# Half of each last down projection by block products: chunks 3 to 6 as two units of seven products of half width

## The chip, the cores and the metric

The kernel is one program on one core of one Trainium2 chip. A core has five engines with an instruction queue each: TensorE (PE in the profile, its weight loads PEld), VectorE (DVE), ScalarE (ACT), GpSimd (POOL) and SyncE (SP, which here only issues transfers). Each queue is worked off in order; an instruction waits at the head of its queue until the semaphores that it names are there. The metric is the device time of one execution in microseconds. Three runs of the kernel before gave 1245.82 to 1248.12 us with a median of 1245.88 us.

## The reference, cut to what matters

Two decoder layers over 512 tokens of width 1024, in float32. Layer 0 mixes by a causal convolution, layer 1 by differential attention; each is followed by a SwiGLU feed-forward part (FFN) of inner width 2816 and by a gated embedding (PLE):

```python
u = rms_norm(h, ffn_norm_g[i])
h = h + (silu(u @ w_gate) * (u @ w_up)) @ w_down
gate = sigmoid(rms_norm(h, ple_norm_g[i]) @ ple_w_gate[i])
h = h + gate * (p[i] @ ple_w_proj[i])
```

The change touches the product with `w_down`, and with it how the PLE part begins.

## The kernel before, in words

**Layout.** Activations lie transposed: a tile `h[c]` holds 128 of the 1024 features in its partitions and the 512 tokens along the free axis, as do the hidden tiles. So the FFN has 22 inner chunks of 128, and every projection has 8 output chunks of 128.

**Three matmuls for one.** Float32 products are made of split operands. Each operand is a rounded part (`hi`) and a rest (`lo`), and `mm3` issues three matmuls, which are L166, L167 and L168 of the profile:

```python
T.matmul(acc, al, bh, start=first, stop=False, **kw)
T.matmul(acc, ah, bh, start=False, stop=False, **kw)
return T.matmul(acc, ah, bl, start=False, stop=last, **kw)
```

For every weight tile of 128x1024 floats there is hence a transfer of 512 KB into `wraw`, a ScalarE cast into `whi` (L159) and a VectorE subtraction into `wlo` (L161). `whi` and `wlo` have four buffers each, `wraw` two.

**The FFN in three parts.** `PARTS` cuts the 22 inner chunks into 6, 8 and 8. The 6 are made plainly. Each 8 are made by *units*: a unit makes two chunks of `u @ w_gate` or of `u @ w_up` by seven block products in place of eight (the scheme of Strassen and Winograd, 2x2 blocks: two chunks of features by two halves of 256 tokens). A unit's seven products are each 4 steps of `mm3` with 128x256 outputs, so 84 matmuls of half width. It needs sums of weight blocks (S1 to S4: four POOL operations of 128x512, L729, L730, L741 and L742) and sums of activation blocks (T1 to T4, made once per layer in `Operands.chunk`). `Unit.prep` makes and splits the weight operands (L719/L720 for two at a time, L745/L746 for S3), `Unit.p` issues a product and drains it. A unit's last two products, 4 and 3, are issued among the next unit's first ones. An up unit's hidden chunks are multiplied with the gate and split into `hid` (L803, L808, L810, L811).

**Down projections.** After each part, `linear` adds `hid @ w_down` to `h`: 8 output chunks, each 8 steps of `mm3` over the part's inner chunks (24 matmuls of 128x512), drained by one VectorE addition from PSUM into `h` (L890). During those of parts 0 and 1 the next part's first unit is prepared; during that of part 2 there is nothing more to prepare, and each finished `h[m]` goes to `Norm.chunk`: a scaled split on ScalarE and VectorE (L206, L207), a square on ScalarE (L225, L228) and its addition to `acc` on POOL (L229).

**PLE.** `ple` makes 8 chunks of 24 matmuls over `norm.u`. After the norm's column sums (L199) and a small chain on VectorE and POOL, two matmuls (L291) spread the token factors over the partitions; ScalarE copies them to `rb` (L262), and only then the first PLE accumulator can be drained (L921, then ScalarE's sigmoid L922). There are four PSUM accumulators `mm`, so the fifth PLE chunk waits for the first drain. `pp`, the eight tiles of `p[i] @ ple_w_proj[i]`, are made well before the FFN and multiplied in at L923.

**What sets the order.** The program is written in the order of the mathematics, and a scheduler, by a timeline of its own, decides the order of each engine's queue. `tc.issue_after` keeps an instruction behind another, and inside `tc.manual_schedule` the written order holds.

Of the kernel before, what the change touches and what calls it, by code (L numbers as in the profile page):

```python
# [91 lines left out]
def trunk(ctx, tc, xT, pT, wts, diag, dww, vec, rel, onehot, lamv, out):  # L92
# [116 lines left out]
    class Norm:  # L209


        def __init__(self, g, acc_engine=None):
            self.g, self.u = g, []
            self.eng = acc_engine or G

        def split(self, c):
            hi, lo = both(sb([P, 2, S], f"A{c}", 1, F32R))
            split_scaled(h[c], col(self.g, c), hi, lo)
            self.u.append((hi, lo))

# [327 lines left out]

    pp = []
    pw = [weight(), weight()]  # L550

# [109 lines left out]
    class Operands:  # L661

        def __init__(self, norm, spare):
            self.norm = norm
            self.tops, self.uppers, lowers = spare()
            self.low = []
            for j in range(2):
                lh, ll = lowers(j)
                self.low += [(lh[:, i], ll[:, i]) for i in range(2)]
            self.at = {n: [None] * 4 for n in ("B11", "B21", "B22", "T1", "T2", "T3", "T4")}  # L670

        def chunk(self, k, rb):
# [13 lines left out]
            V.tensor_tensor(t[:, 3], u21, t[:, 1], ALU.subtract)  # L686
            hi, lo = self.tops(k)
            A.copy(hi, t)
            V.tensor_tensor(lo1, u11, f(hi1), ALU.subtract)
# [8 lines left out]
    class Unit:  # L698
# [9 lines left out]
        def load(self):  # L708
# [6 lines left out]
            self.s3 = sb([P, 2, S], f"A{6 + self.n % 2}", 1)[:, 0]  # L715

        def two(self, src, a, b):
            hi, lo = sb([P, 2, S], "whi", 4, F32R), sb([P, 2, S], "wlo", 4, F32R)
            A.copy(hi, src)  # L719
            V.tensor_tensor(lo, src, f(hi), ALU.subtract)  # L720
            for j, n in enumerate((a, b)):
                self.w[n] = hi[:, j], lo[:, j]

        def prep(self, step):
# [15 lines left out]
            elif step == 3:  # L740
                G.tensor_tensor(s3, r0[:, 0], r1[:, 0], ALU.subtract)  # L741
                G.tensor_tensor(r1[:, 0], r0[:, 1], s[:, 1], ALU.subtract)  # L742
            elif step == 4:
                hi, lo = both(sb([P, 2, S], f"A{4 + self.n % 2}", 1, F32R))
                A.copy(hi, s3)  # L745
                V.tensor_tensor(lo, s3, f(hi), ALU.subtract)  # L746
                self.w["S3"] = hi, lo
            else:
                self.two(r1, "S4", "A22")
# [7 lines left out]
        def p(self, i):  # L757
# [7 lines left out]
            }[i]  # L765
            self.product(acc, w, b, first)
            o = self.out
            if i == 1:
# [6 lines left out]
            elif i == 7:  # L775
                A.copy(o[1][:, HT:], a)
                V.tensor_tensor(o[1][:, HT:], o[1][:, HT:], lo, ALU.add)
                self.ready(1, 1)
# [15 lines left out]
    class Up(Unit):  # L794
        def start(self):
            self.out = wk(), wk()
            self.done = [0, 0]

        def ready(self, j, k):
# [9 lines left out]
            hid = both(sb([P, 2, S], f"B{self.at + j}", 1, F32R))  # L809
            A.copy(hid[0], o)  # L810
            V.tensor_tensor(hid[1], o, f(hid[0]), ALU.subtract)  # L811
            self.hid[self.at + j] = hid

    def ffn(norm, after, spare):
        rb = None
        ops = Operands(norm, spare)

        def units(n, hid):
            us = []
            for i in range(0, n, 2):  # L820
                g, u = Gate(2 * (i // 2), i == 0, "A"), Up(2 * (i // 2) + 1, False, "wraw")
                g.hid = hid
                u.gate, u.at, u.hid = g, i, hid
                us += [g, u]
# [3 lines left out]

        def run(us):
            for n, x in enumerate(us):  # L830
# [6 lines left out]
                if nxt:  # L837
                    nxt.prep(0)
                x.p(2)
                if nxt:  # L840
                    nxt.prep(1)
                if last:
                    last.p(4)
                x.p(6)
                if nxt:
                    nxt.prep(2)
                if last:
                    last.p(3)
                x.p(5)
                if nxt:  # L850
                    nxt.prep(3)
                    nxt.prep(4)
                x.p(7)
                if nxt:
                    nxt.prep(5)
            us[-1].p(4)
            us[-1].p(3)

        us = None
        for at, (f0, n) in enumerate(PARTS):  # L860
# [28 lines left out]
            def add(m, acc):  # L889
                V.tensor_tensor(h[m], acc, h[m], ALU.add)  # L890
                if at == len(PARTS) - 1:
                    after.chunk(m)

            hooks = {}
            if at < len(PARTS) - 1:
                n2 = PARTS[at + 1][1]
                now = wnext[0]
                wnext[0] += NC
                us = units(n2, [None] * n2)
# [47 lines left out]
    n2 = Norm("ple_g0")  # L947
    ffn(norm, n2, spare0)
    norm = Norm("attn_g")
# [323 lines left out]
    n2 = Norm("ple_g1")  # L1273
    ffn(norm, n2, spare1)

# [32 lines left out]
def _layout(a):  # L1308
# [12 lines left out]
    def ffn(i):  # L1321
        g, u = _stationary(a["ffn_w_gate"][i]), _stationary(a["ffn_w_up"][i])
        r = []
        for f0, n in PARTS:
# [3 lines left out]
            for c in range(f0 + plain, f0 + n, 2):  # L1328
                r += [g[c], g[c + 1], u[c], u[c + 1]]
            r += list(pad(_stationary(a["ffn_w_down"][i][f0 * P : (f0 + n) * P])))  # L1330
        return r
# [78 lines left out]
```

## Time and profile before

| | |
|---|---|
| median of 3 runs | 1245.88 us |
| the profiled execution | 1246.42 us, its span 1244.7 us |
| TensorE busy | 1232.4 us, 99% of the span, 7080 matmuls |
| TensorE weight loads | 1080.8 us, 87% |
| VectorE busy | 882.1 us, 71% |
| ScalarE busy | 623.8 us, 50% |
| GpSimd busy | 471.1 us, 38% |
| granted TensorE clock | 1.000 |

The last down projection of layer 0 runs from about 504 to 551 us of the span, and that of layer 1 about 644 us later. A row of a timeline reads: start, duration, engine, line, operation, written tile, read tiles, shape, count, and in brackets how long the engine had been idle and what released it. Names are given without their numbers, so all eight PLE accumulators are `mm`. Matmul durations overlap: what a matmul costs a busy TensorE is the distance from its start to the next one's start.

### The profile page before, as it was taken

How to read it: one execution, taken by the hardware profiler on the slowest of the kernel's cores; microseconds unless marked ns; L12 is line 12 of the kernel's file. 1: busy time of each engine (PE TensorE's matmuls, PEld its weight loads, DVE VectorE, ACT ScalarE, POOL GpSimd, SP SyncE). 2: the span in 40 equal slices, each digit the busy share in tenths (PEclk: the TensorE clock that was granted, in tenths of full speed). 3: DMA queues.
4: the chain of work that ended last, by engine and by line, in shares of the span. 5: the costliest groups of instructions: out<-in, count | busy, mean ns of one | idle time of the engine just before them, and what ended most of it. 6: DMA issues, size and time to landing. Idle time of an engine off the chain costs nothing.

```text
span 1244.7 us, 18430 instructions
## 1 busy us (share of the span) xinstructions
PE 1232.4 (99%) x7080; PEld 1080.8 (87%) x7080; DVE 882.1 (71%) x1242; ACT 623.8 (50%) x1096; POOL 471.1 (38%) x355
## 2 busy tenths in 40 slices
PE   9999999999999999999999999999999999999998
PEld 7888788888998899888888888788889998999887
DVE  6998866885895479547676876646966885587535
ACT  5653464443553255434566877735434552455432
POOL 3863442024670364133346645041026650552120
PEclk9999999999999999999999999999999999999999
DMA  7566213334233322334332331143333333232331
GB/s 267 177 210 193 90 51 119 98 98 127 86 102 118 102 86 71 117 104 149 126 113 76 112 90 38 52 144 93 89 122 95 103 111 112 83 102 86 104 100 67
DMA packets 49154, 136.33 MB, mean 110 GB/s; under 512 B 5635, under 2 KB 10243, under 8 KB 49068
## 3 DMA queue, kind: packets, MB, share of 16 engines
q1 hardware_dynamic: 46944, 131.74, 34.0%
q10 hardware_dynamic: 2124, 3.43, 0.9%
q8 instruction: 55, 0.90, 0.3%
q14 instruction: 31, 0.25, 0.1%
HBM read 128.84 MB, written 6.31 MB: 109 GB/s over the span
## 4 chain that ended last, share of the span: by engine, by line
PE 88%; DVE 4%; issue 2%; DMA 1%; ACT 0%; SPq 0%; POOL 0%; DVEq 0%; ACTq 0%
PE mm L166 27%; PE mm L167 27%; PE mm L168 27%; PE mm L1126 1%; DVE sc L458 1%; PE sc L1094 1%; PE sc L1093 1%; PE tp L1113 1%; PE sc L407 1%; PE mm L407 1%; PE tp L1047 1%; PE mm L363 1%; PE tp L199 1%; DVE wlo L720 0%; DVE wlo L161 0%
## 5 line engine op out<-in xcount | busy, mean ns | idle before, releaser
L159 ACT CAST whi<-wraw 128x1024 fp32r<-128x1024 f32 (+2 forms) x145 | 145.7, 1014 | 229.0 <-PE mm L168 110.9
L161 DVE TENSOR_TENSOR wlo<-wraw,whi 128x1024 fp32r<-128x1024 f32 (+2 forms) x141 | 180.4, 1285 | 82.0 <-ACT whi L159 79.7
L166 PE MATMUL mm<-A,wlo 128*128 128x512 f32 (+1 forms) x568 | 220.4, 388 | 1.1 <-ACT A L206 1.0
L167 PE MATMUL mm<-A,whi 128*128 128x512 f32 (+1 forms) x568 | 219.2, 387 | 0.0
L168 PE MATMUL mm<-A,whi 128*128 128x512 f32 (+1 forms) x568 | 217.3, 389 | 0.0
L166 PE MATMUL mm<-B,wlo 128*128 128x512 f32 x352 | 137.0, 389 | 0.0
L167 PE MATMUL mm<-B,whi 128*128 128x512 f32 x352 | 137.0, 389 | 0.0
L168 PE MATMUL mm<-B,whi 128*128 128x512 f32 x352 | 135.6, 389 | 0.0
L229 POOL TENSOR_TENSOR acc<-acc,wk 128x512 f32<-128x512 f32 x35 | 60.0, 1715 | 190.6 <-ACT wk L228 189.9
L166 PEld LDWEIGHTS mm<-A,wlo 128*128 128x128 f32 x568 | 106.8, 188 | 23.7 <-ACT A L206 1.3
L167 PE MATMUL mm<-C,whi 128*128 128x256 f32 x448 | 126.8, 283 | 0.0
L168 PE MATMUL mm<-C,whi 128*128 128x256 f32 x448 | 126.8, 283 | 0.0
L166 PE MATMUL mm<-C,wlo 128*128 128x256 f32 x448 | 126.8, 283 | 0.0
L168 PEld LDWEIGHTS mm<-A,whi 128*128 128x128 f32 x568 | 106.5, 188 | 21.9 <-issue 0.5
L167 PEld LDWEIGHTS mm<-A,whi 128*128 128x128 f32 x568 | 106.7, 188 | 21.1
L720 DVE TENSOR_TENSOR wlo<-A,whi 128x1024 fp32r<-128x1024 f32 x60 | 106.2, 1778 | 19.7 <-ACT whi L719 19.6
L719 ACT CAST whi<-A 128x1024 fp32r<-128x1024 f32 x60 | 62.9, 1049 | 55.5 <-PE mm L168 44.3
L729 POOL TENSOR_TENSOR A<-A 128x512 f32<-128x512 f32 x16 | 25.7, 1606 | 165.5 <-DMA A<-in_wts 156.7
L729 POOL TENSOR_TENSOR A<-wraw 128x512 f32<-128x512 f32 x16 | 24.7, 1546 | 167.4 <-DMA wraw<-in_wts 152.7
L167 PEld LDWEIGHTS mm<-C,whi 128*128 128x128 f32 x448 | 86.0, 192 | 0.2
L166 PEld LDWEIGHTS mm<-C,wlo 128*128 128x128 f32 x448 | 86.0, 192 | 0.2
L168 PEld LDWEIGHTS mm<-C,whi 128*128 128x128 f32 x448 | 86.0, 192 | 0.0
(314 smaller groups left out, 3031.6 us busy)
## 6 DMA issues: line engine op xcount, KB each, us to landing
wraw<-in_wts SPq DMA_DIRECT2D x161, 512.0 KB, 3.6
A<-in_wts SPq DMA_DIRECT2D x32, 512.0 KB, 3.6
wraw<-in_wts SPq DMA_DIRECT2D x16, 384.0 KB, 3.1
D<-in_diag SPq DMA_DIRECT2D x22, 256.0 KB, 4.8
C<-in_diag SPq DMA_DIRECT2D x16, 256.0 KB, 4.8
h<-in_xT SPq DMA_DIRECT2D x8, 256.0 KB, 5.5
rest<-h SPq DMA_DIRECT2D x8, 256.0 KB, 2.5
bias<-scr ACTq DMA_DIRECT2D x8, 256.0 KB, 3.6
```

Of the source, the lines that this page charges most:

```text
L159: A.copy(hi[:, cut], raw[:, cut])
L161: eng.tensor_tensor(lo[:, cut], raw[:, cut], f(hi[:, cut]), ALU.subtract)
L166: T.matmul(acc, al, bh, start=first, stop=False, **kw)
L167: T.matmul(acc, ah, bh, start=False, stop=False, **kw)
L168: return T.matmul(acc, ah, bl, start=False, stop=last, **kw)
L199: r = T.matmul(t[:, cut], src[:, cut], ones, start=first and b == 0, stop=last and b == 3)
L229: self.last = self.eng.tensor_tensor(self.acc, self.acc, sq, ALU.add)
L363: last_tap[0] = T.matmul(acc, dg[:, j % 4], ups[c][:, j : j + S], start=(j == 0), stop=(j == PE_TAPS[c] - 1))
L407: last_tap[0] = T.matmul(acc[:, g * P : (g + 1) * P], w, ups[c][:, g, LEAD - m : LEAD - m + P], start=(m == 0), stop=(m == LAGS - 1),)
L719: A.copy(hi, src)
L720: V.tensor_tensor(lo, src, f(hi), ALU.subtract)
L729: G.tensor_tensor(s[:, 0], r1[:, 0], r1[:, 1], ALU.add)
```

## The change

Only the third part's down projection of each layer changes.

- Output chunks 0, 1, 2 and 7 are made as before, 24 matmuls of 128x512 each. Chunks 3 and 4, and 5 and 6, are made by one `Down` unit each: seven products of 12 matmuls, 128x256.
- The activation operands are the hidden chunks of part 2 and their block sums. For these the up units of part 2 write their float hidden values where `pp` lay. POOL makes the sums of three of the four chunk pairs (12 operations of 128x256, L924 to L927 of the changed kernel), VectorE those of the fourth (4 operations). Eight ScalarE casts (L933) and eight VectorE subtractions (L934), all 128x512, split them into the tiles of the earlier T1 to T4.
- The weight operands are made as for any unit: two raw tiles, four sums on POOL, four pairs of operands per unit.
- After products 1, 6 and 7, ScalarE copies the accumulator to a `big` tile (L847), since the next product reuses the bank, and VectorE adds it from there to `h` (L920); after the others VectorE adds straight from PSUM.
- `pp` is stored to DRAM after part 0 (8 transfers of 256 KB, L1043) and fetched again behind the second unit's weights (8 of 256 KB, L989).
- PLE reads its operands in the order 0, 1, 2, 7, 3, 4, 6, 5.

The core of the diff:

```diff
+    pps = [[dram.tile([P, S], F32, tag=f"pp{i}{m}", name=f"pp{i}{m}") for m in range(NC)] for i in range(2)]
...
     class Up(Unit):
         def start(self):
-            self.out = wk(), wk()
+            self.out = self.pp[self.at : self.at + 2] if self.pp else (wk(), wk())
...
+    class Down(Unit):
+        def __init__(self, n, m, b, add, done, homes):
+            super().__init__(n, False, None)
+            self.m, self.b, self.add, self.done = m, b, add, done
+            self.homes = homes
+
+        def load(self):
+            self.raw = []
+            r, s, s3, self.thirds = self.homes
+            for j in range(2):
+                raw = sb([P, 2, S], *r[j])
+                self.fetched = nc.sync.dma_start(raw, wts[self.i + j].rearrange("p (j k) -> p j k", j=2))
+                self.raw.append(raw)
+            self.sums = sb([P, 2, S], *s)
+            self.s3 = sb([P, 2, S], *s3)[:, 0]
+
+        def third(self):
+            if len(self.thirds) == 1:
+                return both(sb([P, 2, S], *self.thirds[0], F32R))
+            return [sb([P, S], *t, F32R) for t in self.thirds]
+
+        def start(self):
+            pass
+
+        def drain(self, i, a, lo, hi):
+            t1, t2 = slice(0, HT), slice(HT, S)
+            if i in (1, 6, 7):
+                o = big()[:, :HT]
+                A.copy(o, a)
+            for j, cut, src in {
+                1: lambda: ((0, t1, o),), 2: lambda: ((0, t1, hi),), 6: lambda: ((0, t2, o),), 5: lambda: (),
+                7: lambda: ((1, t2, o), (1, t2, lo)), 4: lambda: ((1, t1, a),), 3: lambda: ((0, t2, lo),),
+            }[i]():
+                self.add(self.m + j, cut, src)
+            if i in (4, 3):
+                self.done(self.m + (i == 4))
...
+        def down(hid, up):
+
+            base = wnext[0]
+            ws = [weight() for _ in range(2)]
+            b = {n: [None] * 4 for n in ("T1", "T2", "T3", "T4")}
+            for n, j, k in (("B11", 0, 0), ("B21", 1, 0), ("B22", 1, 1)):
+                b[n] = [tuple(t[:, k * HT : (k + 1) * HT] for t in hid[2 * i + j]) for i in range(4)]
+
+            def add(m, cut, src):
+                V.tensor_tensor(h[m][:, cut], src, h[m][:, cut], ALU.add)
+
+            def sums(k, eng):
+                (u11, u12), (u21, u22) = ((u[:, :HT], u[:, HT:]) for u in pp[2 * k : 2 * k + 2])
+                eng.tensor_tensor(u22, u22, u12, ALU.subtract)
+                eng.tensor_tensor(u12, u12, u11, ALU.subtract)
+                eng.tensor_tensor(u11, u11, u22, ALU.add)
+                eng.tensor_tensor(u21, u21, u11, ALU.subtract)
+
+            def split(k, i):
+                hi, lo = ops.tiles[k]
+                two = slice(2 * i, 2 * i + 2)
+                src = pp[2 * k + i].rearrange("p (j t) -> p j t", j=2)
+                A.copy(hi[:, two], src)
+                V.tensor_tensor(lo[:, two], src, f(hi[:, two]), ALU.subtract)
+                for j, n in enumerate((("T2", "T1"), ("T4", "T3"))[i]):
+                    b[n][k] = hi[:, 2 * i + j], lo[:, 2 * i + j]
+
+            one = lambda t: (t, 1)
+            xs = [
+                Down(0, 3, b, add, after.chunk, ((one("A6"), one("A3")), one("A4"), one("A7"), (one("A5"),))),
+                Down(1, 5, b, add, after.chunk, ((("wraw", 2),) * 2, one("A6"), one("A3"), (("wth", 2), ("wtl", 2)))),
+            ]
+            x = xs[0]
+            with tc.issue_after(up.last_sum.ins):
+                for k in range(3):
+                    sums(k, G)
+            for i in range(2):
+                xs[i].i = base + 4 + 2 * i
+            wnext[0] = base + 2
+            ws += [weight(), weight()]
+            x.load()
+            x.prep(1)
+            x.prep(3)
+            with behind(up.seventh), tc.manual_schedule(engines={V.engine, A.engine}):
+                for k in range(3):
+                    split(k, 0)
+            with behind(up.ends), tc.manual_schedule(engines={V.engine, A.engine}):
+                sums(3, V)
+                split(3, 0)
+                for k in range(4):
+                    split(k, 1)
+            with behind(up.ends):
+                x.prep(0)
+
+            def plain(ms, ws):
+                accs = [mm() for _ in ms]
+                for k in range(NC):
+                    for w_, a_ in zip(ws, accs):
+                        mm3(a_, wpart(w_, k), hid[k], k == 0, k == NC - 1)
+                for m, a_ in zip(ms, accs):
+                    add(m, slice(0, S), a_)
+
+            plain((0, 1), ws)
+            with behind(x.ends):
+                x.prep(2)
+            for m in range(2):
+                after.chunk(m)
+            plain((2,), ws[2:])
+            with behind(x.ends):
+                x.prep(4)
+                x.prep(5)
+            after.chunk(2)
+            plain((7,), ws[3:])
+            after.chunk(7)
+            wnext[0] = base + 8
+            run(xs, x.ends)
+            with tc.issue_after(xs[1].fetched.ins):
+                for m in range(NC):
+                    nc.sync.dma_start(pp[m], pps[m])
+            after.order = 0, 1, 2, 7, 3, 4, 6, 5
...
-            linear(n, hid, add, 2, at=hooks)
             if hooks:
+                linear(n, hid, add, 2, at=hooks)
                 wnext[0] = end
+            else:
+                down(hid, us[-1])
+            if at == 0:
+                for m in range(NC):
+                    nc.sync.dma_start(pps[m], pp[m])
...
-                for k in range(NC):
-                    mm3(acc, wpart(w, k), tuple(t[:, cut] for t in norm.u[k]), k == 0, k == NC - 1)
+                for k in norm.order:
+                    mm3(acc, wpart(w, k), tuple(t[:, cut] for t in norm.u[k]), k == norm.order[0], k == norm.order[-1])
...
+            if f0 + n == FC:
+                halves = w[3:7].reshape(4, P, 4, 2, P).transpose(0, 1, 3, 2, 4).reshape(4, P, 1024)
+                w = np.concatenate([w[:3], w[7:], halves])
```

How the queues stand afterwards is decided by the scheduler. Three places of layer 0, first in VectorE's queue, from the drain of plain chunks 0 and 1 to the first operand of the second Down unit. `mm_4851` and `mm_4852` are those two accumulators, `wlo_4848`, `wlo_4904` and `wlo_4948` operands of the first Down unit, `wlo_5013` the operand A11 and A12 of the second.

```order
430 L920 TENSOR_TENSOR h_7_87<-mm_4851,h_7_87 128x512
431 L920 TENSOR_TENSOR h_8_88<-mm_4852,h_8_88 128x512
432 L724 TENSOR_TENSOR wlo_4848<-A_750_4811,whi_4847 128x1024
433 L724 TENSOR_TENSOR wlo_4904<-A_752_4815,whi_4903 128x1024
434 L920 TENSOR_TENSOR h_9_89<-mm_4918,h_9_89 128x512
435 L750 TENSOR_TENSOR A_765_4944<-A_753_4816,A_765_4944 128x512
436 L207 SCALAR_TENSOR_TENSOR A_760_4907<-h_7_87,vec_63,A_760_4907 128x512
437 L207 SCALAR_TENSOR_TENSOR A_762_4912<-h_8_88,vec_63,A_762_4912 128x512
438 L724 TENSOR_TENSOR wlo_4948<-A_751_4813,whi_4947 128x1024
439 L207 SCALAR_TENSOR_TENSOR A_768_4951<-h_9_89,vec_63,A_768_4951 128x512
440 L920 TENSOR_TENSOR h_14_94<-mm_4957,h_14_94 128x512
441 L724 TENSOR_TENSOR wlo_5013<-wraw_4989,whi_5012 128x1024
```

Before, the two drains were followed by two weight splits (L161), one drain, three L207 and one more weight split. Now two 128x1024 splits and one 128x512 split are added ahead of `wlo_5013`, which the 25th matmul after the plain chunks reads.

GpSimd's queue at the same place. L733, L734, L745 and L746 are the weight sums (L729, L730, L741 and L742 of before), first of the first Down unit (`A_752` and its neighbours), then of the second (`A_775`, `A_776`, `wraw_4991`); L229 is the norm's sum of squares.

```order
158 L745 TENSOR_TENSOR A_753_4816<-A_750_4811,A_751_4813 128x512
159 L927 TENSOR_TENSOR D_255_1375<-D_255_1375,D_239_1301 128x256
160 L734 TENSOR_TENSOR A_752_4815<-A_752_4815,A_750_4811 128x512
161 L746 TENSOR_TENSOR A_751_4813<-A_750_4811,A_752_4815 128x512
162 L733 TENSOR_TENSOR A_775_4993<-wraw_4991 128x512
163 L734 TENSOR_TENSOR A_775_4993<-A_775_4993,wraw_4989 128x512
164 L229 TENSOR_TENSOR acc_4910<-acc_4910,wk_4915 128x512
165 L229 TENSOR_TENSOR acc_4910<-acc_4910,wk_4954 128x512
166 L745 TENSOR_TENSOR A_776_4994<-wraw_4989,wraw_4991 128x512
167 L746 TENSOR_TENSOR wraw_4991<-wraw_4989,A_775_4993 128x512
168 L229 TENSOR_TENSOR acc_4910<-acc_4910,wk_4986 128x512
```

Before, the L229 additions stood directly behind the last up unit's sums; now 12 activation sums and two units' weight sums stand between and among them. Row 162 writes the tile pair of `A_750`, so it waits for VectorE's row 432.

TensorE's queue at the spread (L291) of the PLE norm of layer 0, before. `mm_5173` is the third PLE accumulator, `mm_5215` the fourth; the fifth, `mm_5257`, begins 24 matmuls after the second spread, at row 2947.

```order
2918 L166 MATMUL mm_5173<-A_792_5056,wlo_5169 128x512
2919 L291 MATMUL tp_5142<-wk_5106,ones_70 128x512
2920 L167 MATMUL mm_5173<-A_792_5056,whi_5168 128x512
2921 L168 MATMUL mm_5173<-A_792_5056,whi_5168 128x512
2922 L291 MATMUL tp_5142<-wk_5108,ones_70 128x512
2923 L166 MATMUL mm_5215<-A_754_4822,wlo_5211 128x512
```

And now, where `mm_5398` is the fourth accumulator and `mm_5440` the fifth.

```order
3015 L167 MATMUL mm_5398<-A_801_5231,whi_5393 128x512
3016 L168 MATMUL mm_5398<-A_801_5231,whi_5393 128x512
3017 L291 MATMUL tp_5325<-wk_5289,ones_70 128x512
3018 L291 MATMUL tp_5325<-wk_5291,ones_70 128x512
3019 L166 MATMUL mm_5440<-A_760_4907,wlo_5436 128x512
```

The chunk of 24 matmuls that stood behind the spread stands ahead of it, and the fifth accumulator follows the spread directly. Layer 1 is ordered alike at these three places.

More of the change, by code (lines that the diff above doesn't have):

```diff
@@ L809, in ready, with third, drain, ffn @@
             hid = both(sb([P, 2, S], f"B{self.at + j}", 1, F32R))
[L810 to L811 removed]
+            self.ends = A.copy(hid[0], o), V.tensor_tensor(hid[1], o, f(hid[0]), ALU.subtract)
             self.hid[self.at + j] = hid
[L814 removed]
+    class Down(Unit):
[12 more added lines that the diff above has]
+            self.s3 = sb([P, 2, S], *s3)[:, 0]
+        def third(self):
+            if len(self.thirds) == 1:
[3 more added lines that the diff above has]
+            pass
+        def drain(self, i, a, lo, hi):
+            t1, t2 = slice(0, HT), slice(HT, S)
[9 more added lines that the diff above has]
+                self.done(self.m + (i == 4))
+    def ffn(norm, after, spare, pp, pps):
         rb = None
         ops = Operands(norm, spare)
[L818 removed]
+        def units(n, hid, last):
             us = []
@@ L827, in units, with run, prep @@
             return us
-        def run(us):
+        def run(us, ends=()):
+            def prep(x, n):
+                with behind(ends):
+                    x.prep(n)
             for n, x in enumerate(us):
```

49 lines of the change are left out of this document (27 added, 22 removed).

## The prediction

> **What bounds the kernel now.** I read the page's busy times and chain of waits first, then the stretches around the last down projection of layer 0, then the timelines there.
>
> ```profile
> span 1244.7 us, 18430 instructions
> PE 88%; DVE 4%; issue 2%; DMA 1%; ACT 0%; SPq 0%; POOL 0%; DVEq 0%; ACTq 0%
> 480.00:505.00 25.00, 25.00 (x207) 24.87 (x206) 19.58 (x24) 15.07 (x26) 7.39 (x4) 1.00 0.27 82
> 505.00:530.00 25.00, 25.00 (x124) 21.15 (x123) 14.66 (x18) 9.81 (x14) 3.28 (x2) 1.00 0.33 104
> 530.00:560.00 30.00, 30.00 (x138) 25.01 (x137) 13.64 (x17) 11.30 (x16) 11.44 (x8) 1.00 0.36 108
> PE sc L407 <- DMA C<-pi: 1.7, 1, 1.7
> ```
>
> The chain is TensorE's. The stretches give busy times of PE, PEld, DVE, ACT and POOL, then the clock: TensorE is busy for all of all three, and the longest wait of the whole run is 1.7 us. So a matmul less is time saved, and any wait put into TensorE's queue here is time lost. From 505 to 560 us VectorE, ScalarE and POOL are half idle, with slack that nothing used. That slack is what the change spends.
>
> **Part 1: the matmuls.** Per layer, 4 x 24 matmuls of width 512 become 2 x 84 of width 256.
>
> ```profile
> 479.91 0.28 PE L168 MATMUL mm<-wtl,whi 128*128 128x256 f32 x1
> 480.03 0.28 PE L166 MATMUL mm<-C,wlo 128*128 128x256 f32 x1
> 534.47 0.69 DVE L890 TENSOR_TENSOR h<-mm,h 128x512 f32<-128x512 f32 x1 [1.53 <-PE mm L168]
> 539.91 0.69 DVE L890 TENSOR_TENSOR h<-mm,h 128x512 f32<-128x512 f32 x1 [2.42 <-PE mm L168]
> ```
>
> Half-width matmuls start 0.12 us apart; VectorE's drains follow each plain chunk 5.44 us apart. A unit takes 84 x 0.12 = 10.08 us in place of 2 x 5.44 = 10.88 us: 0.80 saved, **-1.6 us per layer**. The nearest rows are those of the up units, with the same shapes; nothing would be saved only if the matmuls started 10.88/84 = 0.13 us apart. [...] The rows are 0.227 and 0.12, and I keep to them.
>
> **Part 2: the second Down unit's first operand.** This is the largest term. The second unit's product 1 stands 24 half-width matmuls behind plain chunk 7. Chunk 7 is the fourth chunk and ends where the fourth does now, 534.47 - 5.44 = 529.0; TensorE arrives at 529.0 + 24 x 0.12 = 531.9. It needs `wlo_5013`, row 441 of VectorE's new queue. The rows before:
>
> ```profile
> 514.48 0.69 DVE L811 TENSOR_TENSOR B<-wk,B 128x512 fp32r<-128x512 f32 x1
> 521.10 1.37 DVE L890 TENSOR_TENSOR h<-mm,h 128x512 f32<-128x512 f32 x2 [5.93 <-PE mm L168]
> 522.39 2.35 DVE L161 TENSOR_TENSOR wlo<-wraw,whi 128x1024 fp32r<-128x1024 f32 x2
> 524.65 0.69 DVE L890 TENSOR_TENSOR h<-mm,h 128x512 f32<-128x512 f32 x1
> 525.25 4.15 DVE L207 SCALAR_TENSOR_TENSOR A<-h,vec,A 128x512 fp32r<-128x512 f32 x3
> 479.44 0.68 DVE L746 TENSOR_TENSOR A<-A,A 128x512 fp32r<-128x512 f32 x1
> 487.16 1.45 DVE L746 TENSOR_TENSOR A<-A,A 128x512 fp32r<-128x512 f32 x1
> 494.20 1.22 DVE L720 TENSOR_TENSOR wlo<-A,whi 128x1024 fp32r<-128x1024 f32 x1
> 482.44 4.47 DVE L720 TENSOR_TENSOR wlo<-A,whi 128x1024 fp32r<-128x1024 f32 x2
> 482.30 1.29 POOL L729 TENSOR_TENSOR A<-wraw 128x512 f32<-128x512 f32 x1 [4.80 <-DVE wlo L720]
> 483.56 2.27 POOL L741 TENSOR_TENSOR A<-wraw,wraw 128x512 f32<-128x512 f32 x1
> 488.15 1.62 POOL L742 TENSOR_TENSOR wraw<-wraw,A 128x512 f32<-128x512 f32 x1
> 525.50 3.36 POOL L229 TENSOR_TENSOR acc<-acc,wk 128x512 f32<-128x512 f32 x2 [35.74 <-ACT wk L228]
> ```
>
> VectorE and POOL slow each other: a 128x1024 split takes 1.22 alone and 2.24 beside POOL (4.47 for two), a 128x512 one 0.68 and 1.45, and of the three L207 two stand beside POOL's 3.36 us (at 0.75 for the free one, (4.15 - 0.75)/2 = 1.70 each). POOL's 1.29 becomes 2.27. Additions from PSUM keep 0.69.
>
> VectorE's new work behind the last up unit (free at 514.48 + 0.69) is four 128x256 sums and five 128x512 splits with ScalarE's casts ahead, about 4 x 0.47 + 0.7 + 5 x 0.61 = 5.6 us, with three earlier splits before it (1.8 us) that only partly fit; the drains of 521.10 start about 1.2 us late, at 522.3 (0 to 1.2). From there to the start of `wlo_5013`, start to start and undisturbed: two drains 1.29, two splits 2.26, drain 0.60, split 0.60, two L207 1.34, split 1.14, L207 0.67, drain 0.61, so 8.5 us, to 530.8; the split ends at 532.0. That is a wait of 0.2 us, the low end. Disturbed: POOL may start its row 162 when row 432 is read, at 524.7, and then has 2.27 + 2.27 + 2 x 1.68 + 2.27 + 1.62 = 11.8 us of work, to 536.5. From 524.7 VectorE needs 2.24 + 0.60 + 1.37 + 2 x 1.70 + 2.24 + 1.70 + 0.61 + 2.27 = 14.4 us: 539.1, a wait of 7.2 us, the high end. POOL's list fills 11.8 of the 14.4 us, but its rows 164 and 166 wait for ScalarE and VectorE, so I take three quarters of the way: **+5.4 us**. The cover that fails is VectorE's idle time: it was 2.42 us per chunk, and is gone.
>
> [...]
>
> **Part 3: a copy on the path.** In the first unit product 4 follows product 7 on the same bank, with ScalarE's copy (L847) between. A copy waits for a matmul's end, and product 4 for the copy.
>
> ```profile
> 504.76 0.37 ACT L776 COPY wk<-mm 128x256 f32<-128x256 f32 x1
> 375.08 0.41 DVE L777 TENSOR_TENSOR big<-big,mm 128x256 f32<-128x256 f32 x1
> 375.54 0.39 PE L166 MATMUL mm<-wth,wlo 128*128 128x256 f32 x1 [0.21 <-DVE big L777]
> ```
>
> The last matmul's 0.28 us, some 0.04, the copy's 0.37, 0.05 until TensorE starts (375.49 to 375.54), less the 0.12 that a spacing takes anyway: 0.62 us. A 128x1024 cast of PLE's weight (about 1 us) stands ahead of the copy in ScalarE's queue, so up to 1.6. I take **+1.0 us**.
>
> **Part 4: the fifth PLE accumulator.** It needs the first one's bank, and that needs `rb`. Now 24 matmuls (5.44 us) cover the chain behind the spread:
>
> ```profile
> 568.04 0.39 PE L291 MATMUL tp<-wk,ones 128*128 128x512 f32 x1
> 568.29 1.05 ACT L159 CAST whi<-wraw 128x1024 fp32r<-128x1024 f32 x1 [4.61 <-PE mm L168]
> 569.25 0.58 ACT L262 COPY rb<-tp 128x512 f32<-128x512 f32 x1
> 569.37 1.23 DVE L161 TENSOR_TENSOR wlo<-wraw,whi 128x1024 fp32r<-128x1024 f32 x1 [4.44 <-ACT whi L159]
> 570.52 1.88 DVE L921 TENSOR_TENSOR big<-mm,rb 128x512 f32<-128x512 f32 x3
> ```
>
> In the new order the chunk stands ahead of the spread. From the start of its last matmul: its end 0.39, the cast from 0.43 (its buffer is freed there), `rb` 0.96 later and 0.58 long, VectorE's split 1.08 behind the cast's start, at 1.51, the drain 1.15 later at 2.66, done at 3.35, TensorE at 3.40. Three spacings (0.68) would have passed anyway: **+2.7 us**; without cast and split ahead 1.2, with one more small job 3.
>
> **Part 5: the last up unit.** POOL's twelve new sums now lie beside VectorE's last up unit.
>
> ```profile
> 497.07 0.41 DVE L777 TENSOR_TENSOR big<-big,mm 128x256 f32<-128x256 f32 x1
> 499.82 0.28 PE L166 MATMUL mm<-wth,wlo 128*128 128x256 f32 x1
> ```
>
> That drain frees the bank which the matmul at 499.82 needs: 2.3 us to spare. Right ahead of it in VectorE's queue stand two 128x1024 and two 128x512 instructions with two SBUF inputs; disturbed like those of part 2 they take 2 x 1.02 + 2 x 0.77 = 3.6 us more. POOL's new jobs are half as wide and leave gaps, so I take three quarters, 2.8: **+0.5 us**, between 0 and 1.3.
>
> **At nothing:** the transfers of `pp`,
>
> ```profile
> rest<-h SPq DMA_DIRECT2D x8, 256.0 KB, 2.5
> wraw<-in_wts SPq DMA_DIRECT2D x161, 512.0 KB, 3.6
> ```
>
> which take 2.5 us each beside weights of 3.6 us. The stores pass on SP between loads with waits of their own; the eight loads stand ahead of PLE's first weight, some 20 us before its use, and `pp` itself is read only after 570 us. Without that cover they would cost a few transfers' time. Rows of the attention part that the scheduler sets a little differently: 0, between -1 and +2.
>
> **Sum:** -1.6 + 5.4 + 1.0 + 2.7 + 0.5 = +8.0 us per layer, +16.0 for both. The profiled execution took 1246.4 us and would take 1262.4; the median lies 0.5 below it, so **1262 us**.
>
> **The rivals.** About 0.2% (2.5 us) is what a measurement can tell from no change.
>
> *A. VectorE and POOL find room* (0.16). Part 2 is 0.2, part 5 nothing: -1.6 + 0.2 + 1.0 + 2.7 = +2.3, 1250.5 us. For it: L207 beside no POOL job took 0.75. Against it: in the 480 to 490 us stretch, with POOL's list as dense, every split was slowed. Its lower end, with the small ends of parts 3 and 4, is +0.4, 1246.7 us: no change (0.05 more).
>
> *B. Faster, TensorE waits for nothing* (0.07). The operands come before TensorE, because VectorE, half idle from 505 to 560 us, starts the splits earlier than I count, and the first PLE bank is free at the spread: -1.6 per layer, 1242.7 us. It decides from waits under 0.35 us a layer in all (-1.6 + 0.35 = -1.25, twice that is -2.5). Against it: parts 3 and 4 follow from the order alone.
>
> *C. The clock falls behind the wait* (0.12). At its start TensorE was slow after idling:
>
> ```profile
> 1.52 4.21 PE L141 MATMUL tp<-ones,ident 128*128 128x128 f32 x18 [1.52 <-POOL ident masks.py:199]
> 6.20 1.05 PE L199 MATMUL tp<-ones,wk 128*128 128x128 f32 x8
> ```
>
> 0.23 us a piece, against 0.13 later. A wait of 5.4 us, three times the longest of the trace, may bring that back: 4.2 us at half pace lose 2.1, so 10.1 per layer, 1266 us. The clock stood at 1.00 throughout, so nothing here shows it. [...]
>
> *D. POOL never pauses* (0.08), and each wait is at its high end: 7.2 + 1.6 + 3.0 + 1.3 - 1.6 = 11.5 per layer, 1269 us. For it: the dense rows of 480 to 490 us; against it, POOL's own waits.
>
> **How the numbers follow.** The forecast has 0.52. Faster: B and a rest, 0.08. Same: 0.06. Slower: A to D without these, 0.86. From 1248 to 1270 us stand the forecast and A, C and D, 0.87 before I allow for sizes taken from neighbouring rows, some 0.8 after it; B and no change stay out.
>
> **What would show it.** Right: a wait of 4 to 7 us of TensorE for VectorE's L724 some 28 us behind the last up unit in each layer, with those splits at 2.2 us; one near 1 us for L847; one of 2.7 us for L1057 right behind L291. Half-width matmuls 0.12 us apart show part 1. Wrong: no wait over 1 us at L724 (A or B), or matmuls behind it at twice the spacing (C).

## The result, and the profile after

The changed kernel takes 1267.08 us (median of 5 runs, 1265.73 to 1267.86) against 1246.4 us of the kernel before on the same chip: ratio 1.0164, 95% interval 1.0152 to 1.0177, slower by 20.7 us by the medians, 20.4 by the ratio. The profiled execution's span grew from 1244.7 to 1265.6 us, by 20.9. The forecast was 1262, the range 1248 to 1270.

The page's first line, and of the view of waits the rows on TensorE that are new (line waited at, what for; us in total, times, longest):

```profile
span 1265.6 us, 18932 instructions
PE mm L166 <- DVE wlo L724: 7.8, 2, 3.9
PE mm L166 <- DVE big L1057: 5.2, 2, 2.6
PE mm L166 <- ACT big L847: 1.7, 2, 0.8
```

The three waits of the forecast stand there, each once per layer; no other wait of their size is new. TensorE's timeline of layer 0 shows them from start to start:

```profile
531.65 0.28 PE L168 MATMUL mm<-B,whi 128*128 128x256 f32 x1
535.76 0.58 PE L166 MATMUL mm<-B,wlo 128*128 128x256 f32 x1 [3.82 <-DVE wlo L724]
536.14 0.41 PE L167 MATMUL mm<-B,whi 128*128 128x256 f32 x1
536.35 0.41 PE L168 MATMUL mm<-B,whi 128*128 128x256 f32 x1
...
545.15 0.28 PE L168 MATMUL mm<-C,A 128*128 128x256 f32 x1
546.28 0.39 PE L166 MATMUL mm<-C,wlo 128*128 128x256 f32 x1 [0.84 <-ACT big L847]
...
579.18 0.61 PE L291 MATMUL tp<-wk,ones 128*128 128x512 f32 x2
582.39 0.80 PE L166 MATMUL mm<-A,wlo 128*128 128x512 f32 x1 [2.59 <-DVE big L1057]
582.98 0.63 PE L167 MATMUL mm<-A,whi 128*128 128x512 f32 x1
583.41 0.63 PE L168 MATMUL mm<-A,whi 128*128 128x512 f32 x1
```

The second Down unit's product 1 starts 4.10 us (531.65 to 535.76) behind the matmul ahead of it, 3.98 more than a spacing of 0.12. Behind that, half-width matmuls start 0.21 us apart, and behind the fifth PLE accumulator's wait full-width ones 0.43 apart, where 0.12 and 0.227 were measured at full clock. Three stretches of the first place follow, each with its length, TensorE's busy time (and its matmuls), the granted clock, and the share and GB/s of the transfers:

```profile
532.00:536.00 4.00, 0.24 (x1) 0.75 0.00 0
536.00:538.00 2.00, 2.00 (x10) 0.50 0.31 27
542.00:545.00 3.00, 3.00 (x27) 1.00 0.00 0
```

The granted clock averages 0.75 over the wait, is 0.50 behind it, and 1.00 again in the last stretch. The trace's record of it has the fall at 534.03 us and the rise at 540.86. So a wait here costs twice: while TensorE stands, and while it works at half pace afterwards. The account by the starts of the matmuls, in us:

| | layer 0 | layer 1 |
|---|---|---|
| matmuls saved (2 units x 0.80) | -1.6 | -1.6 |
| wait for L724 (second unit, product 1) | 4.0 | 4.1 |
| half pace behind it (24 and 28 spacings) | 2.3 | 2.7 |
| wait for L847 (copy between products 7 and 4) | 1.1 | 1.1 |
| wait for L1057 (fifth PLE accumulator) | 2.75 | 2.8 |
| half pace behind it (7 and 8 spacings) | 1.4 | 1.7 |
| last up unit | 0 | 0 |
| sum | 10.0 | 10.8 |

Together 20.8, against 20.9 by the spans. The attention part in between added nothing that can be seen.

### The profile page after: what moved, and what is told of

Its sections match the earlier page's. It is cut to its first block, busy times and chain, and to the rows that moved or that the text cites. A ratio compares the mean times of both kernels' runs of the same rounds, so it can differ in the third digit from the quotient of the medians.

```text
span 1265.6 us, 18932 instructions
## 1 busy us (share of the span) xinstructions
PE 1238.6 (98%) x7224; PEld 1092.0 (86%) x7224; DVE 921.6 (73%) x1294; ACT 641.8 (51%) x1132; POOL 527.6 (42%) x395
## 5 line engine op out<-in xcount | busy, mean ns | idle before, releaser
L159 ACT CAST whi<-wraw 128x1024 fp32r<-128x1024 f32 (+2 forms) x137 | 137.2, 1011 | 185.2 <-PE mm L168 70.8
L161 DVE TENSOR_TENSOR wlo<-wraw,whi 128x1024 fp32r<-128x1024 f32 (+2 forms) x133 | 173.4, 1310 | 71.1 <-ACT whi L159 70.7
L166 PE MATMUL mm<-C,wlo 128*128 128x256 f32 x496 | 141.2, 285 | 1.7 <-ACT big L847 1.7
L167 PE MATMUL mm<-C,whi 128*128 128x256 f32 x496 | 140.9, 284 | 0.0
L168 PE MATMUL mm<-C,whi 128*128 128x256 f32 x496 | 140.8, 284 | 0.0
L166 PE MATMUL mm<-B,wlo 128*128 128x512 f32 (+1 forms) x336 | 127.9, 381 | 7.8 <-DVE wlo L724 7.8
L724 DVE TENSOR_TENSOR wlo<-A,whi 128x1024 fp32r<-128x1024 f32 x68 | 115.6, 1710 | 20.6 <-ACT whi L724 20.5
L167 PE MATMUL mm<-B,whi 128*128 128x512 f32 (+1 forms) x336 | 127.3, 379 | 0.0
L168 PE MATMUL mm<-B,whi 128*128 128x512 f32 (+1 forms) x336 | 125.9, 379 | 0.0
L229 POOL TENSOR_TENSOR acc<-acc,wk 128x512 f32<-128x512 f32 x35 | 55.9, 1598 | 129.9 <-ACT wk L228 129.3
L733 POOL TENSOR_TENSOR A<-wraw 128x512 f32<-128x512 f32 x18 | 28.0, 1558 | 196.4 <-DMA wraw<-in_wts 152.8
L724 ACT CAST whi<-A 128x1024 fp32r<-128x1024 f32 x68 | 71.1, 1048 | 57.2 <-PE mm L168 50.1
L166 PEld LDWEIGHTS mm<-C,wlo 128*128 128x128 f32 x496 | 95.9, 193 | 2.4 <-ACT big L847 2.1
L167 PEld LDWEIGHTS mm<-C,whi 128*128 128x128 f32 x496 | 95.8, 193 | 0.3
L733 POOL TENSOR_TENSOR A<-A 128x512 f32<-128x512 f32 x18 | 29.3, 1630 | 160.0 <-DMA A<-in_wts 159.4
L168 PEld LDWEIGHTS mm<-C,whi 128*128 128x128 f32 x496 | 95.7, 193 | 0.0
```

The costliest lines, as they stand in the source:

```text
L159: A.copy(hi[:, cut], raw[:, cut])
L161: eng.tensor_tensor(lo[:, cut], raw[:, cut], f(hi[:, cut]), ALU.subtract)
L229: self.last = self.eng.tensor_tensor(self.acc, self.acc, sq, ALU.add)
L724: self.ends = A.copy(hi, src), V.tensor_tensor(lo, src, f(hi), ALU.subtract)
L733: G.tensor_tensor(s[:, 0], r1[:, 0], r1[:, 1], ALU.add)
```

## The experiments

My theory after the result: three waits, all made by the order and load of VectorE's and ScalarE's queues, and a clock that falls when TensorE stands long enough. The rivals: matmuls that are slow for another reason (operands, banks); a VectorE queue that is too long whatever POOL does; waits that only move when one of them is cleared. In the diffs below `...` stands for lines that are not shown, and the comments explain them.

### Does idling slow TensorE? Needless matmuls in the gaps

```diff
+NF1, NF2 = 17, 11
...
+    def filler(n):
+        t = tp()
+        for _ in range(n):
+            r = T.matmul(t, ones_r, fill_src[0], start=True, stop=True)
+        return r
...
+                    with tc.issue_after(last.second.ins):
+                        filled = filler(NF1)         # ahead of the second Down unit's product 1
+                    with tc.issue_after(filled.ins):
+                        x.p(1)
...
+                with tc.issue_after(last_spread[0].ins):
+                    filled = filler(NF2)             # behind the spread
```

With both:

> 17 needless 128x512 matmuls stand ahead of the second Down unit's product 1, and 11 behind the spread, in each layer; the operands come as late as before. If TensorE's pace behind the waits is lost because it stood idle, the waits of VectorE's chain stay but the matmuls behind them start 0.12 and 0.227 us apart: about 2.5 us less at the first place and 1.5 at the second, twice, so some 8 us off the changed kernel's 1267: 1259. If the slow matmuls have another cause (their operands or their banks), the time stays at 1267 or grows by what the needless matmuls are too many, up to 1 us.

Measured: 1262.1 us, ratio 1.0126 (1.0108 to 1.0145), 5 us under the changed kernel and 3 over what was expected. The matmuls behind both filled gaps ran at full pace. But the scheduler had also put the first unit's product 5 further forward, and it now waited for a drain of VectorE, 2.27 us in each layer. The row of TensorE's timeline in layer 0 and the stretch behind it:

```profile
539.54 0.39 PE L167 MATMUL mm<-C,wlo 128*128 128x256 f32 x1 [2.11 <-DVE h L937]
540.00:542.00 2.00, 2.00 (x12) 0.50 0.02 6
```

In layer 0 that wait brought the clock down again; in layer 1 the same wait (2.39 us from start to start) did not. In the profile the miss is thus 2.27 us twice in place of L847's 1.1, and 1.7 us of half pace once: 2 x 1.2 + 1.7 = 4.1. By the median it is 3.1; the profiled execution, 1263.9 us, is the slowest of four, and two of the others show a mean granted clock of 1.000, so the fall did not come in each. To have the order of the changed kernel untouched, only the second filler was kept:

```diff
-NF1, NF2 = 17, 11
+NF1, NF2 = 0, 11
```

> Of the needless matmuls only the 11 behind the spread stand, in each layer; the rest of TensorE's queue is that of the changed kernel. If idling lowers the pace, the fifth PLE accumulator's matmuls start 0.227 us apart and not 0.43, the wait itself stays: 1.5 us less in layer 0 and 2 in layer 1, 1263.5. If the slow matmuls there come from their operands or banks, they stay slow and the time stays at 1267.

Measured: 1262.9 us, ratio 1.0133 (1.0119 to 1.0146). The timeline behind the spread, layer 0:

```profile
579.08 2.65 PE L705 MATMUL tp<-A,ones 128*128 128x512 f32 x11
581.86 0.50 PE L167 MATMUL mm<-A,wlo 128*128 128x512 f32 x1
582.19 0.40 PE L168 MATMUL mm<-A,whi 128*128 128x512 f32 x1
582.43 0.39 PE L169 MATMUL mm<-A,whi 128*128 128x512 f32 x1
```

The fifth accumulator starts as late as before, 2.8 us behind the spread, but its matmuls are 0.24 apart at once. In the run before it was the same, so behind this filler the clock stood in 4 of 4 cases. The same matmuls on the same operands and bank: it was the idling. The ratios lie 0.0031 apart, 3.9 us, where 1.5 + 2 were expected. Not all of it is the filler's: at the first place, left as it was, half pace cost 1.4 us a layer in this profile and not 2.3 and 2.7.

### Is it POOL that makes the operand late?

```diff
+                w = slice(0, 16 if self.g in ("ple_g0", "ple_g1") else S)
-                self.last = self.eng.tensor_tensor(self.acc, self.acc, sq, ALU.add)
+                self.last = self.eng.tensor_tensor(self.acc[:, w], self.acc[:, w], sq[:, w], ALU.add)
...
+            if self.n == 1:      # sums come from a transfer, POOL writes 16 columns of them
+                nc.sync.dma_start(self.sums, wts[self.i].rearrange("p (j k) -> p j k", j=2))
+                nc.sync.dma_start(self.s3, wts[self.i, :, 0:S])
```

> POOL's weight sums of the second Down unit and the PLE norms' sums of squares are made on 16 of 512 columns (the other columns of the weight sums come from a transfer, the other squares are left out); VectorE's queue is in the same order. If POOL's work is what slows VectorE, its splits take 1.2 and 0.7 us, the 4.0 us wait for L724 falls to 0 to 0.3, and with it the 2.5 us of half pace: 13 us off in two layers, 1254. If the queue is too long by itself, the wait loses less than 1 us and the time stays above 1264.

This kernel leaves out most of both sums and shows times alone. Measured: 1254.4 us, ratio 1.0074 (1.0054 to 1.0094). VectorE's timeline of the changed kernel:

```profile
521.95 1.28 DVE L920 TENSOR_TENSOR h<-mm,h 128x512 f32<-128x512 f32 x2
523.14 2.35 DVE L724 TENSOR_TENSOR wlo<-A,whi 128x1024 fp32r<-128x1024 f32 x2
...
526.01 1.19 DVE L750 TENSOR_TENSOR A<-A,A 128x512 fp32r<-128x512 f32 x1
527.12 3.48 DVE L207 SCALAR_TENSOR_TENSOR A<-h,vec,A 128x512 fp32r<-128x512 f32 x2
530.52 2.31 DVE L724 TENSOR_TENSOR wlo<-A,whi 128x1024 fp32r<-128x1024 f32 x1
532.76 0.74 DVE L207 SCALAR_TENSOR_TENSOR A<-h,vec,A 128x512 fp32r<-128x512 f32 x1
...
534.02 1.68 DVE L724 TENSOR_TENSOR wlo<-wraw,whi 128x1024 fp32r<-128x1024 f32 x1
```

and POOL's beside it:

```profile
524.49 2.16 POOL L733 TENSOR_TENSOR A<-wraw 128x512 f32<-128x512 f32 x1 [14.11 <-DVE wlo L724]
526.73 1.62 POOL L734 TENSOR_TENSOR A<-A,wraw 128x512 f32<-128x512 f32 x1
528.31 3.44 POOL L229 TENSOR_TENSOR acc<-acc,wk 128x512 f32<-128x512 f32 x2
532.91 1.71 POOL L745 TENSOR_TENSOR A<-wraw,wraw 128x512 f32<-128x512 f32 x1 [1.16 <-DVE wlo L724]
```

The same part of VectorE's queue with POOL's work cut to 16 columns:

```profile
526.33 1.41 DVE L207 SCALAR_TENSOR_TENSOR A<-h,vec,A 128x512 fp32r<-128x512 f32 x2
527.66 1.22 DVE L725 TENSOR_TENSOR wlo<-A,whi 128x1024 fp32r<-128x1024 f32 x1
...
530.06 1.22 DVE L725 TENSOR_TENSOR wlo<-wraw,whi 128x1024 fp32r<-128x1024 f32 x1
```

Two L207 take 1.41 us and not 3.48, a split 1.22 and not 2.31, and the late operand is done at 531.3 and not 535.7. The order of VectorE's queue is the same. No wait at product 1 in layer 0, 0.3 us in layer 1, full pace behind it. The wait at product 1 and its share of half pace, 13.1 us in both layers by the account and 12.6 by the times, need POOL's work beside VectorE's.

### Two changes of order alone

The PLE chunk behind the spread again:

```diff
+            if m == 2:
+                return tc.issue_after(columns.ins)        # third accumulator behind the column sums
+            return tc.issue_after(last_spread[0].ins) if m == 3 else nullcontext()
```

> The PLE's third accumulator is put behind the column sums and the fourth behind the spread, so that 24 matmuls stand again between the spread and the fifth accumulator. If the fifth accumulator's wait came from that order alone, the 2.75 us wait and the 1.5 us of slow matmuls behind it go: 8.5 us off, 1258.5. If the chain behind the column sums is then too short of cover, a wait of 1 to 3 us appears at the spread instead, and the time stays above 1262.

Measured: 1259.4 us, ratio 1.0108 (1.0093 to 1.0123). The wait for L1057 and its half pace are gone in both layers, and 0.87 us of waiting in each appeared earlier, at PLE's first accumulator for its last operand (L207).

VectorE's queue eased, with POOL's work as it was:

```diff
-            for m in range(2):
-                after.chunk(m)
...
+            def mid(ins):                 # called behind the second unit's last operands
+                with tc.issue_after(ins.ins):
+                    for m in (0, 1, 2, 7):
+                        after.chunk(m)
```

> The norm's VectorE splits of chunks 0, 1, 2 and 7 (L207) are queued behind the second Down unit's last operands. VectorE then reaches the late operand about 2.5 us earlier: the wait falls from 4.0 to 1.5 us, too short to slow TensorE by the theory of the clock, so 2.5 + 2.5 us less per layer, 10 in all, less some 0.3 of new waits for copies: 1257.5. If the pace falls behind a short wait as well, 1262. If the four L207 are then late for PLE, a wait of 2 us or more appears at PLE's first accumulator and little is won: above 1263.

Measured: 1256.4 us, ratio 1.0084 (1.0065 to 1.0102). The wait at product 1 is gone altogether, better than the 1.5 us expected; the copies cost 1.7 and 0.6 us (1.45 and 0.6 in layer 1) in place of 1.1. So the late operand has two sufficient cures: POOL's work away, or four L207 out of the way. The wait came of both together, not of one. The fifth accumulator's wait stood, 2.7 us long; but here the clock did not fall. Its first matmul in layer 0, and the stretches:

```profile
577.92 0.50 PE L166 MATMUL mm<-A,wlo 128*128 128x512 f32 x1 [2.54 <-DVE big L1061]
...
575.00:578.00 3.00, 0.46 (x3) 1.00 0.58 168
578.00:582.00 4.00, 4.00 (x18) 1.00 0.41 138
```

and the run with POOL's work cut, behind a wait of the same 2.7 us at the same instruction:

```profile
576.00:579.00 3.00, 3.00 (x8) 0.50 0.54 184
```

The same length of wait thus has both outcomes. The profiled execution of the run with the late L207 is the fastest of its four, 1254.8 us; the other three took 1256.1 to 1258.4 with a granted clock of 0.998 or 0.999, so in them it probably fell somewhere, but their traces were not kept.

### All corrections together

The two orders, with two L207 moved half way and ScalarE's cast of PLE's first weight behind the first unit's copy:

```diff
+MID = {2: (0, 1), 5: (2, 7)}              # chunk splits behind these steps of the second unit's prep
...
-            w = weight()
+            w = weight(after=(None, norm.copied if m == 0 else None))
```

> The PLE order of the run before it, the late L207 (two behind the second unit's sums' split, two behind its last operands), and ScalarE's cast of PLE's first weight queued behind the first unit's copy after product 7. If the waits add up as the theory has them, a layer is -1.6 for the matmuls, 0.7 and 0.6 for two copies on the path and 0.2 to 1 at PLE's first accumulator, so -0.1 to +0.7: 1245.5 to 1247. If work that is cleared from one place only moves the wait to another, 1250 or more.

Measured: 1246.4 us, ratio 0.9997 (0.9988 to 1.0006): level with the kernel before. The only new waits left are two copies per layer:

```profile
PE mm L168 <- ACT big L850: 1.8, 4, 0.5
```

Each is 0.74 us from start to start, 0.62 over a spacing, the value of part 3's low end. So a layer is -1.6 + 2 x 0.62 = -0.4. The starts show about another 0.5 us a layer, 0.1 behind each copy and the rest in small waits, which makes it +0.1: level.

With POOL's work cut as well, by the same lines as in the experiment on POOL:

> The same as the one before the last, with POOL's weight sums of the second Down unit and the PLE norms' sums of squares on 16 of 512 columns (the rest comes from a transfer or is left out). With no wait left but two copies of 0.7 and 0.6 us a layer, -1.6 + 1.3 = -0.3 per layer: 1245. If POOL still costs time in the corrected order, this is faster than that by more than 1 us; if not, the same.

Measured: 1247.3 us, ratio 1.0006 (0.9997 to 1.0015), with the same four waits. That is 2.3 us over what was expected and no faster than with POOL's whole work: where VectorE is off the path, what POOL costs it does not show in the time.

Products on one bank kept apart:

```diff
+                if last and ends:
+                    with tc.issue_after(x.last_mm.ins):    # product 4 behind the next unit's product 6
+                        last.p(4)
...
+                with tc.issue_after(x.last_mm.ins) if ends else nullcontext():
+                    x.p(7)                                 # product 7 behind product 5
```

> The same, and products on the same bank kept apart: the second unit's product 6 stands between the first's products 7 and 4. If the copies are what waits there, 0.7 of each layer goes and 0.5 to 1 comes back where product 6 waits for its own copy, 1245 to 1247.5; if the banks do not matter, the time of the run before.

Measured: 1250.7 us, ratio 1.0032 (1.0020 to 1.0043), a miss. Product 6 waited 0.9 us for its own copy, queued on ScalarE behind the first unit's, and then product 3, 1.8 us, for a drain of VectorE:

```profile
PE mm L168 <- DVE h L929: 3.3, 2, 1.7
```

-1.6 + 0.9 + 1.8 + 0.5 and 0.8 of shorter ones is +1.6 and +1.9 in the two layers, 3.5 of the 4.0 us. The profiled execution also shows half pace from 108.9 to 112.3 us, in the convolution, behind a wait for a transfer that stands there in every kernel, 1.4 to 2.3 us from start to start and 2.27 in this one.

The second attempt keeps product 4 behind product 6 and moves the second unit's product 1 and its copy ahead of the first's product 7:

```diff
+                if ends and nxt:
+                    nxt.start()
+                    nxt.p(1)
+                    with tc.issue_after(nxt.copied.ins):
+                        x.p(7)
+                else:
+                    with tc.issue_after(fourth.ins) if ends else nullcontext():
+                        x.p(7)                             # behind the first unit's product 4
```

> The order of the kernel that came out level, and the copies taken off the path: the second unit's product 1 and its copy come before the first's product 7, its product 6 stands between the first's products 7 and 4, and its product 7 behind that product 4. If the two waits of 0.62 us a layer were all that stood against the 1.6 us of matmuls, both layers gain 1.6: 3.2 us below the kernel before, 1243.4, ratio 0.9974. If other waits come in their place, as when the products were moved the first time, no gain: ratio 0.9995 or above.

Measured: 1245.6 us, ratio 0.9986 (0.9977 to 0.9995). Half of what was expected. Both copies are off the path; what is left in each layer is about 0.5 us at a drain, in layer 0:

```profile
541.29 0.39 PE L168 MATMUL mm<-C,wlo 128*128 128x256 f32 x1 [0.39 <-DVE h L939]
```

and by the starts of the matmuls 0.5 and 0.8 of shorter ones. -1.6 + 1.0 and -1.6 + 1.3 are 0.9 us for both layers; measured are 1.7 (0.14% of 1246.9), with an interval from 0.6 to 2.9.

And the four L207 together again:

```diff
-MID = {2: (0, 1), 5: (2, 7)}
+MID = {5: (0, 1, 2, 7)}
```

> The same with all four late L207 behind the second unit's last operands. If nothing queued behind them is waited for, the same time as the one before, 1243.4; if PLE's first accumulator waits for them, up to 1 us a layer more.

Measured: 1245.5 us, ratio 0.9986 (0.9977 to 0.9995); one wait of 0.8 us per layer at a drain in place of the 0.5, and no difference in time. Both intervals end below 1, so these two orders are faster than the kernel before, by about a seventh of a per cent, which is under the 0.2% that I had called the limit of one measurement.

## Why the prediction came out as it did, point by point

**Part 1, the matmuls (-1.6 per layer).** Right. Half-width matmuls were 0.12 us apart wherever the clock was full, and the best order gained what that leaves after its waits, within its interval.

**Part 2, the second unit's operand (+5.4).** Right place, right mechanism, size too large: 4.0 and 4.1. VectorE's drains started at 521.95 and not 522.3. Of the seven instructions that the high end took as disturbed, two kept their undisturbed time: the second of the two splits behind the drains (1.22 us; POOL's first job began behind its start) and the third L207 (0.74, where POOL had stood 1.16 us waiting for VectorE ahead of L745). The late split itself lost 0.46 us and not 1.05 (1.68). I had priced seven instructions as if POOL's list were dense and then taken three quarters of the way by eye. No VectorE instruction here lost more than 1.1 us (the split of 2.31 against 1.22).

**Part 3, the copy (+1.0).** Right, 1.0 and another 0.1 behind it, and for the reason given. ScalarE's timeline shows the weight casts ahead of the copy:

```profile
543.96 1.05 ACT L724 CAST whi<-wraw 128x1024 fp32r<-128x1024 f32 x1 [1.59 <-PE mm L168]
544.91 1.04 ACT L159 CAST whi<-wraw 128x1024 fp32r<-128x1024 f32 x1
545.86 0.64 ACT L847 COPY big<-mm 128x256 f32<-128x256 f32 x2
```

**Part 4, the fifth PLE accumulator (+2.7).** Right: 2.75 and 2.8. The order alone gave it.

**Part 5, the last up unit (+0.5).** Wrong, nothing. VectorE's drain came later than before but not by the 2.3 us that it had to spare:

```profile
498.82 0.41 DVE L783 TENSOR_TENSOR big<-big,mm 128x256 f32<-128x256 f32 x1
```

It stood at 497.07 before; POOL's half-width sums cost VectorE 1.75 us there and not 2.8.

**The step that failed** is the one on the clock. I had the fall of the pace as rival C, with a chance of 0.12 and in place of the forecast, and only behind the longest wait. The sum has no term for it. It came on top of the forecast, behind two waits in each layer: 2.3 and 2.7 us at the first place (C said 2.1) and 1.4 and 1.7 at the second, where I had expected none. Those 8.1 us in two layers are why the time is 1267 and not 1259: without them the smaller part 2 would have put it 3 us under the forecast. What misled me was the sentence that the clock stood at 1.00 throughout. The kernel before had no wait over 1.7 us, so its profile could not say anything on longer ones, and its slow first 18 matmuls were the only row that did. Even there 1.00 was no reading: the trace's record of the clock begins at 5.74 us, where those matmuls end.

**Luck.** That 1267 lies within the range, and 5 us from the forecast, comes in part of errors that cancel. Over both layers parts 2 and 5 were 3.7 us too high and the missing term 8.1 too low, and the upper end of the range was drawn for D's long waits. C's 10.1 us per layer, near the measured 10.0 and 10.8, is near for a like reason: it kept 5.4 us for the first wait and 0.5 for part 5, and had nothing behind the fifth accumulator. The chances are also a little off: 0.87 for 1248 to 1270 is more than the 0.86 for all of slower.

**Rivals A, B and D** did not occur as they stood: VectorE and POOL did not find room, TensorE waited, and POOL did pause. A's condition (POOL not in the way) gave 1254.4 when it was made, where A with the 3.4 us of half pace that this run shows behind part 4 would have been 1250.5 + 3.4 = 1253.9. **Transfers at nothing:** right; no wait of TensorE for a transfer is new.

## What to carry to other kernels

On an engine that never waits, a saving of 1.6 us is smaller than one late operand (4.0 us here): ask first, queue by queue, when each operand of the new work will be ready, and where two products on one bank have another engine between them. A wait in a gapless TensorE stretch is to be priced with the pace behind it, once it is longer than any wait that the trace has; here the clock fell behind as little as 1.88 us of standing, as the last section shows. And the order of queues decided here between 1.6% slower and 0.14% faster with the same work: all of the loss, and the little gain, is in it.

## What the runs showed of the hardware that was not expected

How long TensorE stood, and whether its clock fell behind it, in the profiles of all twelve kernels (start to start of the two matmuls around the gap):

| gap | clock fell behind it |
|---|---|
| 4.1 to 4.5 us (three kernels, both layers) | 6 of 6 |
| 2.9 to 3.0 us (three kernels, both layers) | 4 of 6 |
| 2.0 to 2.4 us (five kernels) | 2 of 6 |
| under 2.0 us | none |

What goes with the one outcome or the other at 2 to 3 us can be read from the traces' records of the granted clock. In the six kernels in which it fell within the work, its 24 changes lie on a grid of 3.413 us, to within 3 ns, and it stayed at 0.50 for one step or two, 3.41 or 6.83 us. In the changed kernel's profile they stand at 534.03, 540.86, 581.82, 585.23, 1189.39, 1196.22, 1237.18 and 1240.59 us, which is 2, 12, 1, 177, 2, 12 and 1 steps from one to the next. I divided all twelve traces by their grids and took, in each step, the time in which no matmul ran:

| TensorE stood, of a step's 3.41 us | clock in the next step |
|---|---|
| at full clock, 1.88 us or more (12 steps) | 0.50, 12 of 12 |
| at full clock, 1.78 us or less (some 4300 steps) | full in all |
| at half clock, 0.82 us or more (4 steps) | 0.50, 4 of 4 |
| at half clock, 0.58 us or less (12 steps) | full, 12 of 12 |

In these traces the outcome thus goes with how a gap lies on the grid. With both fillers, the 2.39 us gap of layer 0 fell into one step, and that of layer 1 into two; these are the steps, with TensorE's busy time:

```profile
536.55:539.96 3.41, 1.30 (x11) 1.00 0.48 155
539.96:543.37 3.41, 3.41 (x18) 0.50 0.01 4
1188.50:1191.91 3.41, 2.54 (x17) 1.00 0.18 24
1191.91:1195.32 3.41, 1.79 (x15) 1.00 0.32 130
1195.32:1198.73 3.41, 3.41 (x31) 1.00 0.17 18
```

TensorE stood for 2.11 us of the one step, and for 0.87 and 1.62 us of the two. This was read from the traces afterwards; no run moved a gap on the grid on purpose, and between 1.78 and 1.88 us nothing was seen.

A fall did not take a step that was idle as a whole: in five of the twelve falls TensorE had stood for only 1.88 to 2.11 us of the step ahead, 55 to 62%.
